# A planner that orders a decoder trunk by itself: which engines keep their order in its urgency rounds, and what it knows of PSUM

## The chip, the cores and the metric

The kernel runs on one core of one Trainium2 chip. The core has a matrix engine (TensorE, PE in the profile; its weight loads are shown apart as PEld), a vector engine (VectorE, DVE), an activation engine (ScalarE, ACT), a general engine (GpSimd, POOL) and a queue engine (SyncE, SP) that here only starts DMAs. Each has its own list of instructions and runs it in order; semaphores make one wait for another. Matmul results land in PSUM, which has eight banks of 128 partitions x 2 KB; everything else lies in SBUF. The metric is the time of one launch on the device in microseconds.

## What is computed

Two layers of a decoder trunk on a sequence of 512 with 1024 features, float32 throughout. Each layer makes one wide projection, runs three token mixers on slices of it (A: top-k sparse attention with an indexer; B: attention in a sliding window; C: stick-breaking attention), and merges them under gates:

```python
mod = c_silu @ w_ada + b_ada
shift, scale, gate = jnp.split(mod, 3, axis=-1)
u = rms_norm(x, norm_g) * (1 + scale[:, None]) + shift[:, None]
z = u @ w_in
(aq, ak, av, ag, iq, ik, iw, bq, bk, bv, bg, cq, ck, cv, cg, ma, mb, mc) = jnp.split(z, SPLIT_OFFSETS, axis=-1)
...
ya = ya.reshape(bsz, seq, A_WIDTH) * jax.nn.silu(ag)
yb = yb.reshape(bsz, seq, B_WIDTH) * jax.nn.silu(bg)
yc = yc.reshape(bsz, seq, C_WIDTH) * jax.nn.silu(cg)
merged = (jax.nn.sigmoid(ma) * (ya @ w_br_a)
          + jax.nn.sigmoid(mb) * (yb @ w_br_b)
          + jax.nn.sigmoid(mc) * (yc @ w_br_c))
return x + gate[:, None] * (merged @ w_out)
...
# stick_breaking_attention, for a block of queries:
z = jnp.einsum('bthd,bshd->bhts', qb, k).astype(jnp.float32) * (dh ** -0.5)
log_beta = jax.nn.log_sigmoid(z)
log_1m = jnp.where(strict, jax.nn.log_sigmoid(-z), 0.0)
after = lax.cumsum(log_1m, axis=3, reverse=True) - log_1m
a = jnp.where(strict, jnp.exp(log_beta + after), 0.0)
```

A final RMS norm follows the second layer.

## The kernel before

**Tiles.** Activations lie with features on partitions and the 512 tokens along the row. A float32 product is made from three matmuls in a faster format: an operand is split into a rounded part and a remainder (`uh`, `ul` for the normed input; `whi`, `wlo` for a weight chunk of 128x512; `yh`, `yl` in one tile `Y`), and high x high, low x high and high x low are summed in one PSUM bank. A weight chunk is loaded into `wstage`, rounded into `whi` (a cast, by ACT, DVE or POOL) and subtracted into `wlo` (DVE or POOL). There are three banks of the name `ps_z`, which take the projections, and five of the name `ps_s`, which take scores, transposes and mixer outputs.

**Stages of a layer.** `first_phase` projects seven column groups while `u` comes about; `v_phase` projects the values; `out_phase` multiplies by `w_out`. Between them the long middle runs several streams at once, woven by `Weave`: the three mixers in the order C, B, A, each for four pairs of heads, and beside them `prep_stream` (projections of queries, keys and gates) and `fill_stream` (merge gates and branch products), whose matmuls of 128x512 fill TensorE.

**A pair of heads in mixer C.** `stack_q` and `stack_k` take a projected bank apart into rounded halves and remainders, in pieces of 64 partitions (`Q`, `KH`, `klow`). `c_qk` makes the scores of the pair in all five `ps_s` banks; for each bank it takes the absolute value, Exp and Ln, a subtraction, a scan along the row (the order lists it as a SCALAR_TENSOR_TENSOR of 128x511, the profile as TENSOR_TENSOR_SCAN) and a last Exp, all in a tile `t`. The scan is the last reader of the bank. `softmax_tr` then transposes `t` in blocks of 128x128 on TensorE (in the profile a matmul `ps_s<-small,t`: the identity lies in `small`) into `ps_s` banks that the scans have set free, and `softmax_pv` multiplies by the values.

**What sets the order.** Nothing is emitted while this code runs: class `Recorder` records every instruction with the tiles it touches and, for many, several engines that could do it (`cast`, `both`). `price` gives a cost for each engine: `cost` is how long the engine is held, `lag` how long until the result can be used. `forward` walks through time: each engine takes the ready instruction with the lowest `prio`, `elsewhere` leaves it if another engine would end it sooner, and a tile's buffer goes to the next tile when its users are done. `latest` goes back through that plan and works out for every instruction the latest time that doesn't delay the end; that becomes its `prio` in the next round. `order` does five rounds, keeps the plan with the earliest end, and `emit` writes each engine's list in that order. All instructions are therefore emitted from line 577 (line 575 for packed pairs of matmuls), and the profile is read by tile names, not by lines.

The framework adds its own semaphore waits when the list is written, whatever the plan believed: instructions of two engines that touch one PSUM tile are kept apart by it. In `add`, the plan knows an order only between accesses that overlap and of which one writes:

```python
over = r[0] < r2[1] and r2[0] < r[1] and r[2] < r2[3] and r2[2] < r[3]
if over and j is not x and (w or w2):
    x.preds[j.i] = j
```

and `latest` hands urgency back along three kinds of link: to what an instruction needs, to the previous user of its buffer, and, for all five engines, to the instruction that stands before it in the engine's list:

```python
if x.engine in after:
    v = min(v, late[after[x.engine]] - x.hold)
```

Of the kernel before, what the change touches and what calls it, by code (L numbers as in the profile page):

```python
# [32 lines left out]
S = 512  # L33
# [214 lines left out]


class Instr:  # L250
    __slots__ = ("i", "alts", "writes", "reads", "preds", "succs", "left", "est", "tiles", "start", "end", "prio", "bound", "engine", "taken", "hold")


class Way:
# [4 lines left out]
class Recorder:  # L259
# [34 lines left out]
    def add(self, ways):  # L294
        x = Instr()
        x.i = len(self.list)
        op, args, kw = next(iter(ways.values()))
        if op == "pairs":
            named = [(("out", "in", "in")[n], v) for q in args for n, v in enumerate(q[:3])]
            opened = {id(q[0]) for q in args if q[3]}  # L300
        else:
            named = [("out" if "out" not in kw and n == 0 else n, v) for n, v in enumerate(args)] + list(kw.items())
        x.writes = [v for n, v in named if isinstance(v, View) and n in ("out", "accum_out")]
        x.reads = [v for n, v in named if isinstance(v, View) and n not in ("out", "accum_out")]
        x.preds, x.succs = {}, []
        for views, w in ((x.reads, False), (x.writes, True)):
            for v, r in [(v, r) for v in views for r in v.regions()]:
                t = v.tile
                if w and (op == "matmul" and kw["start"] or op == "pairs" and id(v) in opened):
                    r = (r[0], r[1], 0, S)  # L310
                keep = []
                for (j, r2, w2) in t.seen:
                    over = r[0] < r2[1] and r2[0] < r[1] and r[2] < r2[3] and r2[2] < r[3]
                    if over and j is not x and (w or w2):
                        x.preds[j.i] = j
                    if not (w and over and r[0] <= r2[0] and r2[1] <= r[1] and r[2] <= r2[2] and r2[3] <= r[3] and j is not x):
                        keep.append((j, r2, w2))
                t.seen = keep + [(x, r, w)]
        x.tiles = list({id(v.tile): v.tile for v in x.reads + x.writes if not v.tile.pool.fixed}.values())
        for j in x.preds.values():  # L320
            j.succs.append(x)
        x.alts = {}
        for e, (op, args, kw) in ways.items():
            x.alts[e] = self.price(x, e, op, args, kw)
        x.prio = x.i
        self.list.append(x)

    def price(self, x, engine, op, args, kw):
# [57 lines left out]
        else:  # L386
# [7 lines left out]
            else:  # L394
                c = 0.1 + 2.35e-3 * n
        y.cost, y.lag = c - self.OVERLAP[engine], c
        return y


    def forward(self):  # L400
# [1 line left out]
        dma_free, lanes = 0.0, []  # L402
        waiting = {}
        for x in self.list:
            x.left, x.est, x.bound, x.taken = len(x.preds), 0.0, len(x.tiles), False
            for t in x.tiles:
                waiting.setdefault(id(t), []).append(x)
        for c in self.classes.values():
# [5 lines left out]
        def offer(x):  # L414
            if x.left == 0 and x.bound == 0:
                for e in x.alts:
                    heapq.heappush(E[e]["pend"], (x.est, x.i))

        def give(c):
            while c.given < len(c.tiles) and c.free:  # L420
# [17 lines left out]
        while len(out) < len(self.list):  # L438
            best = None
            for name, e in E.items():  # L440
# [27 lines left out]
                        elif mine is None:  # L468
                            mine = None
                if mine is not None:  # L470
                    asked = max(free, self.list[mine[2]].est)
                    if best is None or (mine[0], asked, mine) < best[:3]:
                        best = (mine[0], asked, mine, name)
            assert best is not None, "no instruction may go"
# [23 lines left out]
            for s in x.succs:  # L498
                s.est = max(s.est, x.end + self.between(x, s))
                s.left -= 1  # L500
                offer(s)
            for t in x.tiles:
                t.users -= 1
                t.done = max(t.done, x.end + self.CROSS)
                if t.users == 0:
                    heapq.heappush(t.pool.free, (t.done, t.slot))
                    give(t.pool)
# [9 lines left out]
    def elsewhere(self, x, name, at, E):  # L517

        end = at + x.alts[name].cost
        for o, y in x.alts.items():  # L520
            if o != name:
                t = max(E[o]["free"], at, E[o]["port"] if y.port else 0.0) + y.cost
                if t < end - 1e-9:
                    return True
        return False
# [1 line left out]
    def latest(self, end, out):  # L527
# [11 lines left out]
        for x in reversed(out):  # L539
            v = late[x.i]  # L540
            took = x.end - x.start
            for s in x.succs:
                v = min(v, late[s.i] - took - self.between(x, s))
            if x.engine in after:
                v = min(v, late[after[x.engine]] - x.hold)
            for t in x.tiles:
                if id(t) in nxt:
# [57 lines left out]
def trunk(ctx, tc, xT, vecs, w_ss, w_gt, w_first, w_t, w_v, w_br, w_o, rope, consts, out):  # L605
# [268 lines left out]

    def stack_q(r, scale=None, sbuf=True):
        q = rec.tile("Q", [P, 2, S], F32R)
        for e, (a, b) in enumerate(((H0, H1), (H1, H0))):
            if scale is None:
                cast(q[a, e], r[a])
                both(q[b, e], r[a], f(q[a, e]), OP.subtract)  # L880
            else:
                cast(q[a, e], r[a], scale)
                DVE.scalar_tensor_tensor(q[b, e], r[a], scale, f(q[a, e]), op0=OP.mult, op1=OP.subtract)
        return q

# [9 lines left out]
    def stack_k(r, sbuf=True):  # L895
        kh, kl = new_kh(), klow[st["nk"] % 2]
        st["nk"] += 1
        for e, (a, b) in enumerate(((H0, H1), (H1, H0))):
            cast(kh[a, e], r[a])
            cast(kh[b, e], f(kh[a, e]))  # L900
            both(kl[a, :S], r[a], f(kh[a, e]), OP.subtract)
        cast(kl[H1, S:], f(kl[H1, :256]))
        return kh, kl

# [732 lines left out]
```

## Time and profile before

| | us |
|---|---|
| median of three runs | 1181.68 (1181.54 to 1181.86) |
| the profiled execution, launch to end | 1180.98 |
| its span, first to last instruction | 1179.1 |

| engine | busy us in the span | share | instructions |
|---|---|---|---|
| TensorE (PE) | 1166.5 | 99% | 6006 |
| VectorE (DVE) | 988.1 | 84% | 2275 |
| ScalarE (ACT) | 532.0 | 45% | 1127 |
| GpSimd (POOL) | 111.8 | 9% | 160 |

The granted TensorE clock is 0.9 of full speed or more in all 40 slices. The 16 DMA engines are 97% busy in the first 30 us and between 22% and 62% after that. The work on mixer C's pairs of heads lies at 120 to 224 us in the first layer and at 697 to 801 us in the second.

In the timeline a row has the start, the length, the engine and line, the operation, the tile written and the tiles read, the shape, and a count; in square brackets stands how long the engine was idle before it and what ended that. Matmuls overlap in the records: one of 128x512 is shown 0.39 us long, and the next starts 0.23 us after it. What TensorE really loses at a wait is therefore read from start to start, not from the idle time in brackets.

### The profile page before, as it was taken

The page shows a single profiled execution, that of the slowest core. Times are in us where ns is not written, and L with a number is a line of the kernel's source. Part 1 is how long each engine was busy: PE and PEld are TensorE (multiplying, and loading weights), DVE is VectorE, ACT ScalarE, POOL GpSimd, SP SyncE. Part 2 cuts the span into 40 slices and gives each one's busy share as a digit, 9 for nine tenths or more (in the row PEclk, how much of TensorE's full clock was granted, in tenths as well). Part 3 has the DMA queues.
Part 4 walks back from the last instruction along what each step waited for, and adds up shares of the span by engine and source line. Part 5 has one row for each costly group of instructions (what it writes and reads, how often), then busy time and mean ns, then how long its engine had stood idle before and what let it go on. Part 6 is the DMA issues. An engine that isn't in the chain of part 4 may idle for free.

```text
span 1179.1 us, 17734 instructions
## 1 busy us (share of the span) xinstructions
PE 1166.5 (99%) x6006; PEld 967.9 (82%) x6006; DVE 988.1 (84%) x2275; ACT 532.0 (45%) x1127; POOL 111.8 (9%) x160
## 2 busy tenths in 40 slices
PE   9999999999999999999999999999999999999997
PEld 8899777788878887788899987777888888877886
DVE  6977999999999887787587689999997988667765
ACT  6523667653455532632143147775443653234222
POOL 1100333310000000000000014332100000000000
PEclk9999999999999999999999999999999999999999
DMA  9644323334444454245533432333342333322343
GB/s 354 219 119 120 90 81 86 95 107 125 121 116 126 130 143 143 81 141 153 166 113 108 128 101 72 90 87 119 99 132 83 90 98 100 107 72 88 93 125 106
DMA packets 81914, 139.39 MB, mean 118 GB/s; under 512 B 10016, under 2 KB 22560, under 8 KB 81824
## 3 DMA queue, kind: packets, MB, share of 16 engines
q1 hardware_dynamic: 80672, 136.17, 39.5%
q10 hardware_dynamic: 1152, 2.10, 0.5%
q8 instruction: 47, 0.77, 0.3%
q14 instruction: 43, 0.35, 0.1%
HBM read 125.39 MB, written 4.19 MB: 110 GB/s over the span
## 4 chain that ended last, share of the span: by engine, by line
PE 81%; DVE 13%; ACT 2%; issue 2%; DMA 1%; SPq 0%; DVEq 0%; ACTq 0%
PE ps_z L577 61%; PE ps_s L577 16%; DVE t L577 5%; PE ps_s L575 4%; DVE score L577 2%; ACT t L577 1%; DVE m L577 1%; DVE wlo L577 1%; DVE Q L577 1%; DVE klow L577 1%; DMA Y<-in_w_ss 1%; DVE Y L577 0%; DVE wstage L577 0%; ACT KH L577 0%; ACT e L577 0%
## 5 line engine op out<-in xcount | busy, mean ns | idle before, releaser
L577 PE MATMUL ps_z<-uh,whi 128*128 128x512 f32 (+1 forms) x908 | 357.4, 394 | 0.0
L577 PE MATMUL ps_z<-uh,wlo 128*128 128x512 f32 (+1 forms) x908 | 353.4, 389 | 0.0
L577 PE MATMUL ps_z<-ul,whi 128*128 128x512 f32 (+1 forms) x908 | 352.5, 388 | 0.0
L577 DVE TENSOR_TENSOR wlo<-wstage,whi 128x512 fp32r<-128x512 f32 (+2 forms) x321 | 210.4, 659 | 11.0 <-ACT whi L577 2.3
L577 PEld LDWEIGHTS ps_z<-uh,whi 128*128 128x128 f32 x908 | 170.5, 188 | 35.2 <-issue 1.9
L577 PEld LDWEIGHTS ps_z<-uh,wlo 128*128 128x128 f32 x908 | 170.6, 188 | 34.6 <-issue 0.9
L577 PEld LDWEIGHTS ps_z<-ul,whi 128*128 128x128 f32 x908 | 170.7, 188 | 32.6 <-issue 0.7
L577 DVE CAST whi<-wstage 128x512 fp32r<-128x512 f32 (+2 forms) x224 | 91.3, 408 | 106.6 <-PE ps_z L577 87.5
L577 PE MATMUL ps_z<-Y,whi 128*128 128x512 f32 x384 | 119.3, 391 | 0.0
L577 ACT CAST whi<-wstage 128x512 fp32r<-128x512 f32 (+2 forms) x105 | 63.2, 602 | 109.9 <-PE ps_z L577 82.3
L577 ACT ACTIVATE e<-ps_z 128x512 f32<-128x512 f32 x68 | 40.3, 592 | 135.9 <-PE ps_z L577 135.7
L577 POOL TENSOR_TENSOR wlo<-wstage,whi 128x512 fp32r<-128x512 f32 (+2 forms) x51 | 64.8, 1271 | 382.7 <-ACT whi L577 143.8
L577 ACT ACTIVATE e<-e 128x512 f32<-128x512 f32 x96 | 59.8, 629 | 53.3 <-DVE e L577 52.8
L577 PEld LDWEIGHTS ps_z<-Y,whi 128*128 128x128 f32 x384 | 71.7, 188 | 14.7
L577 ACT ACTIVATE t<-t,nm 128x256 f32<-128x256 f32 (+3 forms) x128 | 65.1, 510 | 35.5 <-DVE nm L577 35.5
L577 PE MATMUL ps_z<-Y,wlo 128*128 128x512 f32 x192 | 74.7, 389 | 0.0
L577 ACT ACTIVATE t<-t 128x512 f32<-128x512 f32 x120 | 68.2, 625 | 13.3 <-DVE t L577 12.5
L577 PEld LDWEIGHTS ps_s<-small,t 128*128 128x128 f32 x432 | 48.8, 140 | 16.2 <-DVE t L577 5.1
L577 PE MATMUL ps_s<-small,t 128*128 128x128 f32 x432 | 58.2, 275 | 3.6 <-DVE t L577 2.5
L577 DVE MAX8 m<-score 128x8 f32<-128x256 f32 (+2 forms) x96 | 53.3, 556 | 1.1
L577 PE MATMUL ps_s<-KH,Q 128*128 128x256 f32 (+3 forms) x280 | 52.4, 309 | 0.2
L577 DVE MATCH_REPLACE8 score<-m,score 128x256 f32<-128x256 f32 (+2 forms) x96 | 52.1, 543 | 0.1
(202 smaller groups left out, 1951.5 us busy)
## 6 DMA issues: line engine op xcount, KB each, us to landing
wstage<-in_w_t SPq DMA_DIRECT2D x212, 256.0 KB, 2.7
wstage<-in_w_v SPq DMA_DIRECT2D x48, 182.0 KB, 2.4
Y<-in_w_ss SPq DMA_DIRECT2D x16, 512.0 KB, 6.2
m<-zs SPq DMA_DIRECT2D x128, 64.0 KB, 2.0
wstage<-in_w_gt SPq DMA_DIRECT2D x32, 256.0 KB, 2.6
wstage<-in_w_ss SPq DMA_DIRECT2D x32, 256.0 KB, 2.7
wstage<-in_w_o SPq DMA_DIRECT2D x32, 256.0 KB, 2.7
wstage<-in_w_first SPq DMA_DIRECT2D x16, 256.0 KB, 4.4
```

Source lines behind the costliest of these rows:

```text
L575: self.real[engine].matmul(*[real(a) for a in q[:3]], start=q[3], stop=True, skip_group_check=True)
L577: made = getattr(self.real[engine], y.op)(*[real(a) for a in y.args], **{k: real(v) for k, v in y.kw.items()})
```

## The change

Six edits, five of them in the planner:

1. `add`: two accesses to one PSUM tile, one by TensorE and one by another engine, of which one writes, are ordered even where they touch different columns (`bank and mine != ...`). Two accesses by engines other than TensorE that don't depend on each other are noted in `after` and `apart`: if they go to different engines, the later waits for the end of the earlier; on one engine they follow without a gap (`soft`).
2. `price`: an instruction of ACT or DVE on fewer than 128 partitions holds its engine for its full length and 0.02 or 0.08 us more; before, the overlap with its successor was taken off.
3. `elsewhere`: another engine's start is worked out from when the instruction is ready, not from when this engine could take it. An engine that is idle early is found more often.
4. `latest`: urgency goes back along an engine's list for TensorE and the loads (SP) only; DVE, ACT and POOL may be put in another order in the next round.
5. `latest` also goes back along the `apart` links.
6. `stack_q` and `stack_k` are recorded with all rounded halves ahead of the remainders, where the two halves of 64 partitions used to be written one after the other.

```diff
+        mine = next(iter(ways)) == "PE"
...
+                bank = t.pool.name[:3] == "ps_"
                 for (j, r2, w2) in t.seen:
                     over = r[0] < r2[1] and r2[0] < r[1] and r[2] < r2[3] and r2[2] < r[3]
-                    if over and j is not x and (w or w2):
+                    if j is not x and (w or w2) and (over or bank and mine != ("PE" in j.alts)):
                         x.preds[j.i] = j
+                    elif j is not x and bank and not mine and "PE" not in j.alts:
+                        x.after[j.i] = j
...
+            x.after.pop(j.i, None)
+        for j in x.after.values():
+            j.apart.append(x)
...
         y.cost, y.lag = c - self.OVERLAP[engine], c
+        if engine != "POOL" and o.shape[0] < P:
+            y.cost = c + (0.08 if engine == "DVE" else 0.02)
...
-            x.left, x.est, x.bound, x.taken = len(x.preds), 0.0, len(x.tiles), False
+            x.left, x.est, x.bound, x.taken = len(x.preds) + len(x.after), 0.0, len(x.tiles), False
+            x.soft = {}
...
-                    heapq.heappush(E[e]["pend"], (x.est, x.i))
+                    heapq.heappush(E[e]["pend"], (max(x.est, x.soft.get(e, 0.0)), x.i))
...
+            for s in x.apart:
+                for o in s.alts:
+                    if o != name:
+                        s.soft[o] = max(s.soft.get(o, 0.0), x.end + self.NEXT)
+                s.left -= 1
+                offer(s)
...
-                t = max(E[o]["free"], at, E[o]["port"] if y.port else 0.0) + y.cost
+                t = max(E[o]["free"], x.est, x.soft.get(o, 0.0), E[o]["port"] if y.port else 0.0) + y.cost
...
+            for s in x.apart:
+                v = min(v, late[s.i] - (x.hold if s.engine == x.engine else took + self.NEXT))
-            if x.engine in after:
+            if x.engine in after and x.engine in ("PE", "SP"):
                 v = min(v, late[after[x.engine]] - x.hold)
...
-        for e, (a, b) in enumerate(((H0, H1), (H1, H0))):
+        sides = tuple(enumerate(((H0, H1), (H1, H0))))
+        for e, (a, b) in sides:
             cast(kh[a, e], r[a])
+        for e, (a, b) in sides:
+            both(kl[a, :S], r[a], f(kh[a, e]), OP.subtract)
+        for e, (a, b) in sides:
             cast(kh[b, e], f(kh[a, e]))
-            both(kl[a, :S], r[a], f(kh[a, e]), OP.subtract)
```

Every matmul, load and vector operation of the kernel stays; their order on each engine changes, and for some the engine. TensorE's list differs in small exchanges at a few dozen places. POOL goes from 165 to 196 instructions, DVE from 2101 to 2061 and ACT from 1009 to 1018, counted in the orders. Three places are shown; the number at a row's start is its place in the engine's list, `xN` a repetition.

**TensorE in mixer C, first layer, second pair of heads**, where the transposes of `t` start between the matmuls of a projection (`ps_z`). Before:

```order
750 L577 MATMUL ps_z<-uh_607,wlo 128x512
751 L577 MATMUL ps_s<-small,t 128x128 x13
752 L577 MATMUL ps_z<-uh_206,whi 128x512
753 L577 MATMUL ps_z<-ul_221,whi 128x512
754 L577 MATMUL ps_s<-small,t 128x128 x3
755 L577 MATMUL ps_z<-uh_206,wlo 128x512
756 L577 MATMUL ps_z<-uh_268,whi 128x512
```

and now:

```order
748 L595 MATMUL ps_z<-uh_605,wlo 128x512
749 L595 MATMUL ps_s<-small,t 128x128 x11
750 L595 MATMUL ps_z<-uh_222,whi 128x512
751 L595 MATMUL ps_s<-small,t 128x128 x2
752 L595 MATMUL ps_z<-ul_232,whi 128x512
753 L595 MATMUL ps_z<-uh_222,wlo 128x512
754 L595 MATMUL ps_z<-uh_266,whi 128x512
755 L595 MATMUL ps_z<-ul_294,whi 128x512
756 L595 MATMUL ps_s<-small,t 128x128 x3
```

The group of three stood behind 13 transposes and two matmuls; it now stands behind 13 transposes and five matmuls, three later.

**VectorE in mixer C, first layer, fourth pair of heads**, from the second subtraction to the last scan (128x511). Before:

```order
279 L577 TENSOR_TENSOR m_2251<-m_2251,rt 128x512
280 L577 SCALAR_TENSOR_TENSOR t<-ps_s,t 128x511
281 L577 MEMSET t 128x1
282 L577 SCALAR_TENSOR_TENSOR t<-ps_s,t 128x512 x2
283 L577 TENSOR_TENSOR zc<-zc,m_2251 128x512
284 L577 SCALAR_TENSOR_TENSOR t<-ps_s,t 128x511
285 L577 MEMSET t 128x1
286 L577 SCALAR_TENSOR_TENSOR t<-ps_s,t 128x511
287 L577 SCALAR_TENSOR_TENSOR t<-ps_s,t 128x512 x2
288 L577 TENSOR_TENSOR KH<-zc,KH 64x512 x3
289 L577 SCALAR_TENSOR_TENSOR t<-ps_s,t 128x511
```

and now:

```order
278 L595 SCALAR_TENSOR_TENSOR t<-ps_s,t 128x512 x2
279 L595 SCALAR_TENSOR_TENSOR t<-ps_s,t 128x511 x2
280 L595 SCALAR_TENSOR_TENSOR t<-ps_s,t 128x512 x2
281 L595 SCALAR_TENSOR_TENSOR t<-ps_s,t 128x511 x2
282 L595 SCALAR_TENSOR_TENSOR t<-ps_s,t 128x512
283 L595 TENSOR_TENSOR zc<-ps_z,rt 128x512
284 L595 SCALAR_TENSOR_TENSOR t<-ps_s,t 128x511
```

The five operations on `m`, `zc` and `KH`, which belong to mixer B's keys, stood between the scans; one other stands there now, and the memsets have gone to POOL.

**VectorE in mixer C, first layer, between the projections of the first pair of heads and its first absolute value.** Before:

```order
164 L577 CAST KH<-ps_z 64x512
165 L577 CAST KH<-KH 64x512
166 L577 TENSOR_TENSOR klow_80<-ps_z,KH 64x512 x2
167 L577 MAX m_1428<-score_1256 128x8
168 L577 CAST whi<-wstage 128x512
169 L577 MATCH_REPLACE score_1256<-m_1428,score_1256 128x256
170 L577 TENSOR_TENSOR wlo<-wstage,whi 128x512
171 L577 MAX m_1457<-score_1256 128x8
172 L577 TENSOR_SCALAR mods_76<-dotg,small 128x1
173 L577 MATCH_REPLACE score_1256<-m_1457,score_1256 128x256
174 L577 MAX m_1473<-score_1256 128x8
175 L577 MATCH_REPLACE score_1256<-m_1473,score_1256 128x256
```

and now:

```order
169 L595 TENSOR_TENSOR wlo<-wstage,whi 128x512
170 L595 CAST KH<-KH 64x512
171 L595 TENSOR_TENSOR klow_80<-ps_z,KH 64x512 x2
172 L595 MAX m_1439<-score_1256 128x8
173 L595 TENSOR_TENSOR wlo<-wstage,whi 128x512
174 L595 MATCH_REPLACE score_1256<-m_1439,score_1256 128x256
175 L595 MAX m_1467<-score_1256 128x8
176 L595 MATCH_REPLACE score_1256<-m_1467,score_1256 128x256
```

One cast of `KH` out of the bank has gone to ACT. From the last score of the indexer (row 151 before, 157 now) to the first absolute value of the pair, the list has six MAX and six MATCH_REPLACE of the top-k search before, four and four now; three `whi` casts before, one now; two `wlo` before, four now.

More of the change, by code (lines that the diff above doesn't have):

```diff
@@ L250 @@
 class Instr:
-    __slots__ = ("i", "alts", "writes", "reads", "preds", "succs", "left", "est", "tiles", "start", "end", "prio", "bound", "engine", "taken", "hold")
+    __slots__ = ("i", "alts", "writes", "reads", "preds", "succs", "left", "est", "tiles", "start", "end", "prio", "bound", "engine", "taken", "hold", "after", "apart", "soft")
 class Way:
@@ L304, in add @@
         x.reads = [v for n, v in named if isinstance(v, View) and n not in ("out", "accum_out")]
-        x.preds, x.succs = {}, []
+        x.preds, x.succs, x.after, x.apart = {}, [], {}, []
+        mine = next(iter(ways)) == "PE"
         for views, w in ((x.reads, False), (x.writes, True)):
@@ L470, in forward @@
                 if mine is not None:
-                    asked = max(free, self.list[mine[2]].est)
+                    asked = max(free, self.list[mine[2]].est, self.list[mine[2]].soft.get(name, 0.0))
                     if best is None or (mine[0], asked, mine) < best[:3]:
@@ L876, in stack_q @@
         q = rec.tile("Q", [P, 2, S], F32R)
-        for e, (a, b) in enumerate(((H0, H1), (H1, H0))):
+        sides = tuple(enumerate(((H0, H1), (H1, H0))))
+        for e, (a, b) in sides:
+            cast(q[a, e], r[a], scale)
+        for e, (a, b) in sides:
             if scale is None:
-                cast(q[a, e], r[a])
                 both(q[b, e], r[a], f(q[a, e]), OP.subtract)
             else:
-                cast(q[a, e], r[a], scale)
                 DVE.scalar_tensor_tensor(q[b, e], r[a], scale, f(q[a, e]), op0=OP.mult, op1=OP.subtract)
@@ L897, in stack_k @@
         st["nk"] += 1
-        for e, (a, b) in enumerate(((H0, H1), (H1, H0))):
+        sides = tuple(enumerate(((H0, H1), (H1, H0))))
+        for e, (a, b) in sides:
             cast(kh[a, e], r[a])
+        for e, (a, b) in sides:
+            both(kl[a, :S], r[a], f(kh[a, e]), OP.subtract)
+        for e, (a, b) in sides:
             cast(kh[b, e], f(kh[a, e]))
-            both(kl[a, :S], r[a], f(kh[a, e]), OP.subtract)
         cast(kl[H1, S:], f(kl[H1, :256]))
```

## The prediction

> **What bounds the kernel now.** I read the page's busy times first, then the list of who waited for whom, then the timeline at each wait.
>
> ```profile
> PE 1166.5 (99%) x6006; PEld 967.9 (82%) x6006; DVE 988.1 (84%) x2275; ACT 532.0 (45%) x1127; POOL 111.8 (9%) x160
> PE ps_s L577 <- DVE t L577: 2.5, 7, 0.6
> PE ps_s L577 <- ACT t L577: 1.1, 2, 0.6
> PE ps_s L577 <- DVE vc L577: 0.6, 1, 0.6
> PE ps_s L577 <- ACT e L577: 0.2, 1, 0.2
> ```
>
> TensorE is busy 99% of the span, so whatever the planner does to other engines counts only where TensorE waits, at its start or behind its last matmul. The rows from the list of waits (time in total, times, longest) say where that is: nine waits for the tile `t`, which is what `softmax_tr` transposes, 3.6 us together, and one at the start. Since matmuls overlap, a wait costs more than the idle time. For five of the nine the timeline of TensorE has:
>
> ```profile
> 135.42 0.40 PE L577 MATMUL ps_z<-uh,wlo 128*128 128x512 f32 x1
> 136.46 0.41 PE L577 MATMUL ps_s<-small,t 128*128 128x128 f32 x2 [0.64 <-DVE t L577]
> 161.56 0.40 PE L577 MATMUL ps_z<-ul,whi 128*128 128x512 f32 x1
> 162.24 0.55 PE L577 MATMUL ps_s<-small,t 128*128 128x128 f32 x3 [0.29 <-DVE t L577]
> 162.54 0.48 PE L577 MATMUL ps_z<-uh,wlo 128*128 128x512 f32 x1
> 162.86 0.39 PE L577 MATMUL ps_z<-uh,whi 128*128 128x512 f32 x1
> 163.09 0.40 PE L577 MATMUL ps_z<-ul,whi 128*128 128x512 f32 x1
> 186.21 0.40 PE L577 MATMUL ps_z<-ul,whi 128*128 128x512 f32 x1
> 186.80 0.55 PE L577 MATMUL ps_s<-small,t 128*128 128x128 f32 x3 [0.19 <-DVE t L577]
> 209.11 0.27 PE L577 MATMUL ps_s<-small,t 128*128 128x128 f32 x1
> 209.93 1.10 PE L577 MATMUL ps_s<-small,t 128*128 128x128 f32 x8 [0.54 <-ACT t L577]
> 210.78 0.48 PE L577 MATMUL ps_z<-uh,whi 128*128 128x512 f32 x1
> 492.84 0.39 PE L577 MATMUL ps_z<-Y,wlo 128*128 128x512 f32 x1
> 493.47 1.33 PE L577 MATMUL ps_s<-small,t 128*128 128x128 f32 x10 [0.25 <-DVE t L577]
> 713.46 0.41 PE L577 MATMUL ps_s<-small,t 128*128 128x128 f32 x2 [0.64 <-DVE t L577]
> ```
>
> Without a wait the next start comes 0.23 us after a matmul of 128x512 (162.86 to 163.09). From 135.42 to 136.46 are 1.04 us, so 0.81 is lost; likewise 0.45 at 162.24, 0.36 at 186.80, 0.40 at 493.47. Eight transposes take from 209.93 to the next matmul at 210.78, a step of 0.11 us, so 0.71 is lost at 209.93. Each loss is the idle time and about 0.16 us of overlap; for all nine that makes 3.6 + 9 x 0.16 = **5.0 us**. The row at 713.46 shows the first of them again in the second layer, with the same idle time to the hundredth: the two layers have the same plan in this stage. Everything else on TensorE is matmuls at their pace, and the change neither removes nor adds one. So the ceiling of the gain is about 5 us, 0.4% of the span, with what the start may give on top.
>
> The stage around the first four waits, in the table by stretches (columns PE, PEld, DVE, ACT and POOL busy, clock, DMA share, GB/s), and the vector engine just ahead of it:
>
> ```profile
> 120.00:224.00 104.00, 102.34 (x554) 79.12 (x553) 102.44 (x204) 70.75 (x128) 38.93 (x56) 1.00 0.32 89
> 105.36 0.16 DVE L577 TENSOR_SCALAR iw<-ps_s 128x4 f32<-128x4 f32 x1 [0.34 <-ACT va L577]
> 105.85 0.16 DVE L577 TENSOR_SCALAR iw<-ps_s 128x4 f32<-128x4 f32 x1 [0.33 <-ACT va L577]
> 115.57 0.67 DVE L577 TENSOR_SCALAR Q<-ps_z 64x512 fp32r<-64x512 f32 x1
> 116.27 0.59 ACT L577 ACTIVATE Q<-ps_z 64x512 fp32r<-64x512 f32 x1 [0.42 <-DVE Q L577]
> 116.90 1.39 DVE L577 SCALAR_TENSOR_TENSOR Q<-ps_z,Q 64x512 fp32r<-64x512 f32 x2 [0.27 <-ACT Q L577]
> ```
>
> VectorE is as full as TensorE there, 102.4 of 104 us, so its order decides when `t` is ready. It waits for ACT where no data passes: `iw` and `va` are different columns of one bank, the two pieces of `Q` different partitions of one. The old plan took these pairs for simultaneous, so its VectorE ran late against plan. And two instructions on 64 partitions last 1.39 us, twice 0.69: the overlap that the old price takes off isn't there.
>
> **The change part by part.** The plan now counts those waits and prices (edits 1 and 2), so it places TensorE's transposes later and the scans earlier. Place by place, for the first layer:
>
> Second and third pair of heads. The group of three that waits at 162.24 moves behind three more matmuls, 3 x 0.23 = 0.69 us against a loss of 0.45. At the third pair the same group moves behind two more, 0.46 against 0.36. Gain 0.45 and 0.36, if VectorE is no later than before.
>
> First pair. TensorE's order ahead of the wait is the old one, so the gain must come from VectorE. Its durations in this stage (groups by shape, count, busy time and mean):
>
> ```profile
> L577 DVE MAX8 m<-score 128x8 f32<-128x256 f32 x14 | 5.9, 424 | 0.2
> L577 DVE MATCH_REPLACE8 score<-m,score 128x256 f32<-128x256 f32 x14 | 5.7, 410 | 0.0
> L577 DVE MATCH_VALUE_LOAD score<-m,score 128x8 f32 x22 | 1.9, 88 | 0.4
> L577 DVE CAST KH<-ps_z 64x512 fp32r<-64x512 f32 x1 | 0.7, 694 | 0.0
> L577 DVE CAST whi<-wstage 128x512 fp32r<-128x512 f32 x3 | 1.2, 411 | 0.0
> L577 DVE TENSOR_TENSOR wlo<-wstage,whi 128x512 fp32r<-128x512 f32 x8 | 5.4, 680 | 0.0
> ```
>
> Ahead of the first absolute value two MAX go (0.85), two MATCH_REPLACE with their loads (1.00), two `whi` casts (0.82), one `KH` cast (0.69), and two `wlo` come (1.36); one `whi` cast comes behind it (0.41). That is 1.6 us less in front of the scan that TensorE waits for. Of this 0.81 is needed: gain 0.81.
>
> Fourth pair. The old list has five operations of other mixers between the second subtraction and the last scan of the pair (the order above), and the timeline has their lengths:
>
> ```profile
> 202.49 0.68 DVE L577 TENSOR_TENSOR m<-m,rt 128x512 f32<-128x512 f32 x1
> 205.43 0.68 DVE L577 TENSOR_TENSOR zc<-zc,m 128x512 f32<-128x512 f32 x1
> 209.59 2.09 DVE L577 TENSOR_TENSOR KH<-zc,KH 64x512 fp32r<-64x512 f32 x3
> ```
>
> That is 0.68 + 0.68 + 2.09 = 3.45 us; one `zc` product, about 0.7, stands there now. So the last scan comes 2.7 us earlier in the list, and TensorE's transposes spread: one, then four matmuls, two, and so on, where nine stood together. Gain 0.71.
>
> The wait at 493.47 (mixer A): its transposes move behind three more matmuls, 0.69 against 0.40. In the second layer the C waits come again, 2.33, and the A wait is smaller (nine waits at 5.0 in all, less 2.33 twice and 0.40, which leaves next to nothing). Sum of the gains, if every one comes whole: 2.33 + 2.33 + 0.40 = **5.1 us**, the ceiling but for rounding.
>
> Against it stands what the new order makes late elsewhere. Two bounds from the rows: nothing, or nine new waits like the old ones, 5.0 us. A few hundred VectorE positions change, while the plan is wrong by less; I take a quarter of the old, 1.2 us, near the lower end, because the kinds of wait that surprised the old plan are the ones now counted.
>
> The start. The four warming matmuls on `vc` now stand ahead of the first sum of squares, not behind it:
>
> ```profile
> 13.54 0.67 PE L577 MATMUL ps_s<-t,nones 128*128 128x256 f32 x2 [0.62 <-DVE vc L577]
> 14.04 1.05 PE L577 MATMUL ps_s<-vc,nones 128*128 128x128 f32 x8
> 21.89 0.76 DVE L577 TENSOR_TENSOR ul<-e,uh 128x256 fp32r<-128x256 f32 x2
> 22.99 0.28 PE L577 MATMUL ps_z<-ul,whi 128*128 128x256 f32 x1
> ```
>
> That sum waits for both products `vc`, since it writes their bank; half the warming matmuls need only the first, so up to 0.45 us is won. But VectorE takes over a `wlo` of 128x384 (0.5) from POOL, and a `ul` (0.4) comes behind a long product, ahead of the `ul` at 21.89. That one was ready at 22.3 and used at 22.99: 0.7 us of slack, less the 0.45 won. Between a gain of 0.45 and a loss of 0.6 I take zero.
>
> The end. VectorE's `m` and `xm` change places with two output products, but the last chain starts at the last projection matmul, which is unmoved: nothing either way. `stack_q` and `stack_k` (edit 6) have the same instructions; their order is in the lists already counted. The loads keep their order but for a few that change places by one or two; with DMA at 0.32 in the stage they have room, at 0.97 in the first 30 us less, which is in the bounds of the start.
>
> Sum: 5.1 - 1.2 + 0 = 3.9 us less than the profiled execution's 1180.98 (span 1179.1 and 1.9 around it), 1177.1; against the median of the runs, which is 0.7 above that execution, 1181.68 - 3.9 = **1177.8 us**.
>
> **The rivals.** *The waits move on (0.24).* The plan's list scheduler never meant to wait before either, and it still did nine times. With VectorE full, earlier scans push other work back, and the lateness shows up at another transposing or at a projected bank. Half the waits or more come back: a gain of 0 to 2.3 us, about 1180.5. For it speaks 102.44 of 104; against it that top-k work has room behind mixer C, where VectorE is less full (84% over the whole span).
>
> *POOL holds VectorE up (0.12, slower).* POOL gets 31 instructions more. Its subtraction is long:
>
> ```profile
> L577 POOL TENSOR_TENSOR wlo<-wstage,whi 128x512 fp32r<-128x512 f32 x18 | 23.3, 1294 | 24.4 <-DVE KH L577 8.3 <-DVE whi L577 6.8 <-DVE wlo L577 3.3
> ```
>
> If VectorE's operations on SBUF can't run beside it, one such subtraction started just ahead of a cast or `wlo` that a scan stands behind delays the scan by up to 1.29 us. It decides once the delay exceeds the half microsecond that the transposes were moved. With one in each of the eight pairs of heads: 8 x (1.29 - 0.5) = 6.3 us of new waits, less the 3.9, +2.4: about 1184. In the trace of before POOL starts behind VectorE, as the row's releasers say, and such pairs don't overlap, which speaks for the lock but also for a plan that respects it. The Trainium skill says of this (SBUF — State Buffer, "Who interferes with whom") that the port pair is an exclusive lock and that whichever engine issues first makes the other block for the whole instruction. By that rule the sum would depend on who comes first; the trace agrees so far as POOL's idle time is ended by VectorE.
>
> *The plan guards too much.* If engines could read two halves of a bank at once, edit 1 would buy needless gaps. The row at 116.27 decides: ACT waited 0.42 us for the other 64 partitions of the bank. The Trainium skill (PSUM — Partial Sum Buffer, "PSUM bank collisions raise a hardware error") says that accesses in different quadrants of one bank may go at the same time; by it those 0.42 us would be free. Here the kernel's own semaphores make the wait, whole bank by whole bank, so the plan's rule fits the trace and the sum stands.
>
> *All comes, and the start as well (0.07):* 5.1 + 0.45, 1176.1.
>
> **How the numbers follow.** The forecast has 0.57: 1176.5 to 1179.2. A measurement of this kernel tells about 0.2% from no change, 2.4 us, so faster ends at 1179.3. The forecast and the last rival lie below it: faster 0.64; the waits moving on is within: 0.24; POOL: slower 0.12. The range of 8 in 10 goes from 1175.8, nearly the ceiling, to 1182.0, which takes in the waits moving on and leaves out POOL's case.
>
> **What would show it.** In the new list of waits the rows of TensorE for `t` should fall from 3.6 us in 9 to about 1 us in 2 or 3, with none over 0.6. In the timeline the third scan of the first pair should end a microsecond before the transposes behind it start. TensorE's busy time should fall little, since the matmuls are the same. I am wrong if the nine waits go and the time stays: then TensorE loses pace somewhere that the list of waits doesn't show, and the starts of its matmuls have to be laid side by side. I am wrong in size if more than three waits of over 0.3 us stand at new places, and wrong in sign if VectorE is idle behind POOL in the stage of mixer C.

## The result, and the profile after

| | before | after |
|---|---|---|
| median, us (6 runs each) | 1181.75 | 1174.03 |
| ratio, 95% interval | | 0.9936 (0.9923 to 0.9948) |
| the profiled execution (span), us | 1180.98 (1179.1) | 1174.64 (1172.5) |

The change makes the kernel 7.7 us faster; 3.9 us were forecast, and 1174.03 lies below the range. All runs of one kernel, here and below, lie within 2.2 us of one another, but for one of e8's five, which took 4073 us and is left out of its ratio. The page's busy times after, and the list of whom TensorE waited for (total, times, longest):

```profile
PE 1162.2 (99%) x6006; PEld 968.4 (83%) x6006; DVE 981.1 (84%) x2235; ACT 536.1 (46%) x1136; POOL 127.9 (11%) x191
PE ps_s L595 <- DMA wstage<-in_w_first: 1.4, 1, 1.4
PE ps_s L595 <- DVE epst L595: 1.0, 1, 1.0
PE ps_s L595 <- ACT e L595: 0.6, 1, 0.6
PE ps_s L595 <- DVE vc L595: 0.2, 1, 0.2
```

All nine waits for `t` are gone, and the list shows nothing in their place between start and end. TensorE's busy time fell from 1166.5 to 1162.2 us, 4.3 us, while its idle time (span less busy) fell only from 12.6 to 10.3, by 2.3. The 1.4 us row, a wait for a load at the start, is new and luck, as shown below; behind the first 20 us the idle time fell by 3.3. So over half of what went had stood in the records as busy time.

To see where, the same instruction is looked up in both timelines. First the start and the end: VectorE's first product on `Y`, which needs the first chunk of a weight load, and the last two sums on TensorE. Before, then after:

```profile
9.23 1.23 DVE L577 SCALAR_TENSOR_TENSOR Y<-Y,csr 128x1024 f32<-128x1024 f32 x1 [4.17 <-DMA Y<-in_w_ss]
1171.56 0.70 PE L577 MATMUL ps_s<-e,nones 128*128 128x256 f32 x2 [0.21 <-ACT e L577]
```

```profile
10.33 1.23 DVE L595 SCALAR_TENSOR_TENSOR Y<-Y,csr 128x1024 f32<-128x1024 f32 x1 [5.34 <-DMA Y<-in_w_ss]
1164.88 0.70 PE L595 MATMUL ps_s<-e,nones 128*128 128x256 f32 x2 [0.59 <-ACT e L595]
```

The load landed 1.1 us later in the profiled execution of the changed kernel, although the loads stand in the same order up to there in both kernels. Counted from that product to the last sums, the time went from 1162.33 to 1154.55 us, 7.78 less. This **inner time** leaves the luck of the first load out, and for the change it agrees with the medians; I use it beside them below. Now the stages between. Before (first scores ahead of mixer C, the first products with mixer B's values `vb` behind it, then the same in the second layer):

```profile
105.16 0.28 PE L577 MATMUL ps_s<-KH,Q 128*128 128x256 f32 x1
242.75 1.74 PE L575 MATMUL ps_s<-t,vb 128*64 128x256 f32 x16
682.16 0.28 PE L577 MATMUL ps_s<-KH,Q 128*128 128x256 f32 x1
819.77 1.73 PE L575 MATMUL ps_s<-t,vb 128*64 128x256 f32 x16
```

and after:

```profile
106.09 0.28 PE L595 MATMUL ps_s<-KH,Q 128*128 128x256 f32 x1
240.54 1.73 PE L593 MATMUL ps_s<-t,vb 128*64 128x256 f32 x16
678.83 0.28 PE L595 MATMUL ps_s<-KH,Q 128*128 128x256 f32 x1
813.31 1.73 PE L593 MATMUL ps_s<-t,vb 128*64 128x256 f32 x16
```

| stretch, between these rows | gain, us | of it at transposes | forecast, without the 1.2 given back |
|---|---|---|---|
| first product on `Y` to first scores | 0.17 | – | 0 |
| mixer C, first layer | 3.14 | 2.60 | 2.33 |
| rest of the first layer | 1.12 | 0.95 | 0.40 |
| mixer C, second layer | 3.13 | 2.63 | 2.33 |
| rest of the second layer | 0.22 | 0.47 | 0 |
| sum | 7.78 | 6.65 | 5.1 |

The gains are differences of the starts above (for mixer C of the first layer, from +0.93 to -2.21). The third column compares, for each of the 432 transposes, the step from the start of the matmul ahead with the median step between the same two shapes, and sums what is over by 0.025 us or more: 7.0 us at 40 starts before, 0.35 at 4 after. Ten starts lost over 0.15 us each, 5.2 together; the other thirty lost 0.025 to 0.12, 1.8 together. These thirty are in no list of waits. TensorE's timeline at one of them, before:

```profile
138.65 0.39 PE L577 MATMUL ps_z<-uh,whi 128*128 128x512 f32 x1
138.99 0.55 PE L577 MATMUL ps_s<-small,t 128*128 128x128 f32 x3
139.29 0.48 PE L577 MATMUL ps_z<-ul,whi 128*128 128x512 f32 x1
```

and the same group after:

```profile
138.11 0.39 PE L595 MATMUL ps_z<-uh,wlo 128*128 128x512 f32 x1
138.34 0.49 PE L595 MATMUL ps_s<-small,t 128*128 128x128 f32 x3
138.59 0.47 PE L595 MATMUL ps_z<-uh,whi 128*128 128x512 f32 x1
```

Before, the transposes start 0.34 us behind the matmul ahead (0.23 after) and take 0.30 (0.25 after). No bracket marks this, since the matmul ahead was still shown running. The group of all transposes, before and after (count, busy time and mean of one, idle time ahead):

```profile
L577 PE MATMUL ps_s<-small,t 128*128 128x128 f32 x432 | 58.2, 275 | 3.6 <-DVE t L577 2.5 <-ACT t L577 1.1
```

```profile
L595 PE MATMUL ps_s<-small,t 128*128 128x128 f32 x432 | 57.5, 272 | 0.0
```

The idle time shows 3.6 of the 7.0 us.

The same comparison at all other starts finds one loss that the new order has added, in mixer A of the second layer. TensorE before, then after:

```profile
1070.03 1.33 PE L577 MATMUL ps_s<-small,t 128*128 128x128 f32 x10
1071.25 0.50 PE L577 MATMUL ps_z<-uh,whi 128*128 128x512 f32 x1
```

```profile
1063.14 1.25 PE L595 MATMUL ps_s<-small,t 128*128 128x128 f32 x10
1064.54 0.50 PE L595 MATMUL ps_z<-uh,whi 128*128 128x512 f32 x1
```

Ten transposes without a wait and the step to the next matmul take 1.0 us; after, it starts 1.40 us behind the first of them, since ACT still reads the projected bank (`e<-ps_z`, 1063.91 to 1064.48). That is 0.39 us, of which 0.14 are idle time, too short for a bracket. It is the main reason why the rest of the second layer gained less than its transposes.

### The profile page after: what moved, and what is told of

Its sections match the earlier page's. It is cut to its first block, busy times and chain, and to the rows that moved or that the text cites. A ratio compares the mean times of both kernels' runs of the same rounds, so it can differ in the third digit from the quotient of the medians.

```text
span 1172.5 us, 17783 instructions
## 1 busy us (share of the span) xinstructions
PE 1162.2 (99%) x6006; PEld 968.4 (83%) x6006; DVE 981.1 (84%) x2235; ACT 536.1 (46%) x1136; POOL 127.9 (11%) x191
## 4 chain that ended last, share of the span: by engine, by line
PE 97%; issue 1%; ACT 1%; DMA 1%; DVE 1%; SPq 0%; DVEq 0%
PE ps_z L595 73%; PE ps_s L595 19%; PE ps_s L593 5%; DMA Y<-in_w_ss 1%; ACT t L595 0%; DVE Y L595 0%; DVE t L595 0%; SPq L595 0%; ACT e L595 0%; ACT ps_s L595 0%; ACT whi L595 0%; DVE wlo L595 0%; DVE xm L595 0%; DVE vc L595 0%; DVEq L1653 0%
## 5 line engine op out<-in xcount | busy, mean ns | idle before, releaser
L595 DVE TENSOR_TENSOR wlo<-wstage,whi 128x512 fp32r<-128x512 f32 (+2 forms) x331 | 218.4, 661 | 12.0 <-ACT whi L595 1.9
L595 DVE CAST whi<-wstage 128x512 fp32r<-128x512 f32 (+2 forms) x231 | 94.6, 410 | 114.0 <-PE ps_z L595 95.9
L595 ACT CAST whi<-wstage 128x512 fp32r<-128x512 f32 (+2 forms) x112 | 67.7, 604 | 132.8 <-PE ps_z L595 106.9
L595 POOL TENSOR_TENSOR wlo<-wstage,whi 128x512 fp32r<-128x512 f32 (+2 forms) x41 | 52.2, 1273 | 143.8 <-DVE whi L595 60.2
```

The costliest lines, as they stand in the source:

```text
L595: made = getattr(self.real[engine], y.op)(*[real(a) for a in y.args], **{k: real(v) for k, v in y.kw.items()})
```

## The experiments

Twelve kernels ran, each beside runs of the kernel before on the same chip. "Inner" is the time from the first product on `Y` to the last sums in the one profile of each, against 1162.33 before. It lies within 0.7 us of the medians but for e4, e6 and e10, where the two differ by 0.9 to 1.3.

| kernel | median (us against before) | ratio, 95% interval | inner against before |
|---|---|---|---|
| the change | -7.7 | 0.9936 (0.9923 to 0.9948) | -7.8 |
| e1 edit 4 alone | -0.7 | 0.9992 (0.9983 to 1.0001) | -1.0 |
| e2 all but edit 4 | -4.4 | 0.9962 (0.9950 to 0.9975) | -4.4 |
| e3 before, TensorE's list new | +5.2 | 1.0044 (1.0031 to 1.0056) | +5.1 |
| e4 changed, TensorE's list old | +4.8 | 1.0039 (1.0025 to 1.0053) | +3.5 |
| e5 all but edits 1 and 5 | -4.9 | 0.9960 (0.9948 to 0.9972) | -4.6 |
| e6 all but edit 2 | -5.3 | 0.9959 (0.9947 to 0.9972) | -4.3 |
| e7 all but edit 6 | -8.5 | 0.9930 (0.9917 to 0.9944) | -7.8 |
| e8 all but edit 3 | -8.0 | 0.9931 (0.9918 to 0.9945) | -7.7 |
| e9 edits 1, 2, 4, 5 | -7.6 | 0.9936 (0.9924 to 0.9949) | -7.7 |
| e10 changed, VectorE's list kept in `latest` | -4.7 | 0.9962 (0.9949 to 0.9974) | -3.7 |
| e11 changed, ACT's list kept in `latest` | -8.2 | 0.9933 (0.9919 to 0.9947) | -7.7 |
| e12 all but the `elif` of edit 1, and 5 | -6.1 | 0.9951 (0.9939 to 0.9964) | -6.3 |

My theory at first was that of the prediction: TensorE waited because the plan did not know the pairs on one bank and the 64-row prices (edits 1 and 2). The rival: the freed urgency (edit 4) is the gain.

**e1: edit 4 alone**, against the kernel before.

```diff
-            if x.engine in after:
+            if x.engine in after and x.engine in ("PE", "SP"):
```

> The kernel before with edit 4 alone: urgency goes back along the lists of TensorE and the loads only; banks and 64-row prices as the old plan knows them. Knowledge theory (TensorE waited because the plan did not know the pairs on one bank and the 64-row prices): the plan still believes the scans come earlier than they do, so most of the nine waits for t stay, more than 2.5 of 3.6 us in the list of waits, and the time is within 1.5 us of before. Urgency theory (the old order of VectorE was frozen by handing urgency back along its own list, and freeing it is the gain): the waits for t fall under 1 us and the time is 5 to 8 us below before. If each brings a part, 2 to 5 us below.

TensorE's waits in it:

```profile
PE ps_s L589 <- DVE t L589: 1.6, 6, 0.3
PE ps_s L589 <- DVE zc L589: 1.6, 2, 0.8
PE ps_s L589 <- ACT t L589: 0.6, 1, 0.6
```

Waits for `t` fall from 3.6 to 2.2 us, where the first theory expected more than 2.5 to stay and the rival less than 1, and two for `zc` come, 1.6 us. A plan that is free to reorder but works with wrong prices trades one wait for another. A gain can't be told from none (the interval includes 1). The rival falls as the whole cause.

**e2: all but edit 4.**

```diff
-            if x.engine in after and x.engine in ("PE", "SP"):
+            if x.engine in after:
```

> The changed kernel with edit 4 undone: the plan knows banks and 64-row prices, urgency goes back along all five lists as before. Knowledge theory: the waits for t stay away and the time is within 1.5 us of the changed kernel, 6 to 8 us below before. Urgency theory: the plan sees the lateness but can't reorder VectorE against its last round; waits for t of 2.5 us and more, and a time within 2 us of before. If each brings a part, 2 to 5 us below before.

Mixer C has no wait left. All that stands between start and end is in mixer A, at three places (timeline):

```profile
490.53 1.33 PE L595 MATMUL ps_s<-small,t 128*128 128x128 f32 x10 [0.28 <-DVE t L595]
492.96 0.50 PE L595 MATMUL ps_z<-uh,whi 128*128 128x512 f32 x1 [1.10 <-ACT e L595]
1067.43 1.39 PE L595 MATMUL ps_s<-small,t 128*128 128x128 f32 x10 [0.97 <-ACT t L595]
```

These are 0.44, 1.34 and 1.13 us from start to start, 2.9 of the 3.3 us by which its inner time is over that of the change. Knowledge alone brings over half, and gives back at a new place what it can't order there. Both theories were half right: each brings a part.

**e3 and e4: TensorE's list exchanged.** Is the gain TensorE's, whose transposes stand later, or VectorE's, whose scans stand earlier? e3 is the kernel before with TensorE's list rearranged into the order of the planner's edits, the other lists word for word as before; e4 the changed kernel with TensorE's list in the old planner's order. Read from the traces, e3's list is not that of the change (210 of 6006 places differ, all but two of them in mixer C's stages) but that of e7 and e9 below, two versions without edit 6 that are as fast as the change; e4's differs in 150 places from that of before.

```diff
+MOVED = {25: [60, 61, 63, 64, 73], 79: [184, 151, 152, 154, 155, 157, 158, 160, 161, 163, 164, 166, 167, 169, 170], ...
...
+        for n, ids in MOVED.items():
+            assert sorted(lists["PE"][n:n + len(ids)]) == sorted(ids)
+            lists["PE"][n:n + len(ids)] = ids
```

> The kernel before with TensorE's list alone in the order of the changed planner (57 small exchanges); VectorE, ACT, POOL and the loads stand as before. Theory that TensorE's own order is enough (transposes two or three matmuls later): gain at the second and third pairs and at mixer A, 2 x (0.45 + 0.36) + 0.40, about 2 us, the first pair's 0.8 stays. Theory that VectorE's order is what counts: the scans end when they did, the waits move from one transposing to another, and the time is within 1 us of before or above it.

> The changed kernel with TensorE's list alone in the old planner's order (51 small exchanges back); the other engines stand as changed. Theory that VectorE's order is what counts: most of the gain stays, 5 us or more below before, with waits for t under 1.5 us. Theory that TensorE's own order is what counts: waits for t of 2 us or more, and less than half of the gain, under 4 us below before.

Both are some 5 us slower than before, which neither theory had forecast for e4; for e3 the second had only "or above it". In e3 TensorE's new list asks for what the old lists of the other engines deliver late:

```profile
139.17 0.55 PE L623 MATMUL ps_s<-small,t 128*128 128x128 f32 x3 [0.40 <-ACT t L623]
210.44 1.20 PE L623 MATMUL ps_s<-small,t 128*128 128x128 f32 x9 [1.21 <-ACT t L623]
```

In e4 the old list has the scores of the second pair two projection matmuls earlier; they need a bank that VectorE's `e` reads last, and VectorE now has `e` later:

```profile
149.34 0.47 PE L641 MATMUL ps_s<-KH,Q 128*128 128x256 f32 x2 [2.40 <-DVE e L641]
```

It comes again in the second layer. Part of e4's time is the clock's. Its trace has the granted clock at half for 3.4 us behind the first of these waits (columns: PE, PEld, DVE, ACT and POOL busy, clock, DMA share, GB/s):

```profile
151.30:154.70 3.40, 3.40 (x10) 2.66 (x9) 2.14 (x5) 3.12 (x7) 0.00 (x0) 0.50 0.21 66
```

Matmuls of 128x512 start 0.43 us apart there in place of 0.23, which costs about 1.7 us of the profiled run. All five runs of e4 have a mean granted clock of 0.995 to 0.997, those of before 0.998 or 0.999. Even without the 1.7 us the inner time is 1.8 over that of before.

The same list of TensorE is 5 us slower than before beside the old lists (e3) and 8 us faster beside new ones (e7, e9). So the gain does not lie in TensorE's list alone, and by e4 not in the other lists alone, but in that they fit each other.

**e5 and e6: which knowledge.** e5 takes the banks out (edits 1 and 5; the loop of edit 5 is not shown), e6 the price (edit 2).

```diff
-                    if j is not x and (w or w2) and (over or bank and mine != ("PE" in j.alts)):
+                    if j is not x and (w or w2) and over:
...
-                    elif j is not x and bank and not mine and "PE" not in j.alts:
-                        x.after[j.i] = j
```

```diff
-        if engine != "POOL" and o.shape[0] < P:
-            y.cost = c + (0.08 if engine == "DVE" else 0.02)
```

> The changed kernel without the knowledge of shared banks (edits 1 and 5 undone); the 64-row price, the freed urgency and edits 3 and 6 stay. If bank knowledge is what ends the waits of mixer C: waits for t of 1.5 us and more come back as in the kernel with edit 4 alone, and the time is within 3 us of before. If the 64-row price is enough: waits for t under 0.7 us, time 6 to 8 us below before. If each brings a part: 3 to 6 below.

> The changed kernel without the 64-row price (edit 2 undone); all else stays. If bank knowledge is enough: time within 1 us of the changed kernel, 6.5 to 8 us below before, waits for t under 0.7 us. If the price is what counts: waits for t of 1.5 us and more, time within 3 us of before. If each brings a part: 3 to 6 below.

Each brings a part, and of different waits. Without banks there is hardly a wait in mixer C, but there are others where TensorE meets VectorE on a bank (e5; the one for `zc` is there in both layers):

```profile
58.60 0.57 PE L591 MATMUL ps_s<-whi,uh 128*128 128x364 f32 x2 [0.30 <-DVE zc L591]
331.16 1.16 PE L591 MATMUL ps_s<-KH,Q 128*128 128x256 f32 x8 [0.41 <-DVE mx L591]
```

Without the price the first pair's wait is back, 0.69 from start to start in each layer where it was 0.81, and the scores of the second pair wait 0.83 (e6):

```profile
136.25 0.41 PE L593 MATMUL ps_s<-small,t 128*128 128x128 f32 x2 [0.52 <-DVE t L593]
148.22 0.51 PE L593 MATMUL ps_s<-KH,Q 128*128 128x256 f32 x2 [0.58 <-DVE e L593]
```

**e7, e8 and e9: edits 3 and 6.** e7 has `stack_q` and `stack_k` as before, e8 `elsewhere`, e9 both.

```diff
-                t = max(E[o]["free"], x.est, x.soft.get(o, 0.0), E[o]["port"] if y.port else 0.0) + y.cost
+                t = max(E[o]["free"], at, E[o]["port"] if y.port else 0.0) + y.cost
```

> The changed kernel with stack_q and stack_k recorded in the old way (edit 6 undone). If the gain is the plan's, which orders these pieces by itself from the banks it knows: within 1 us of the changed kernel, 7 to 8 us below before. If writing all halves out of the bank first shortens VectorE's path to the scans: waits for t come back at the pairs of mixer C, and 1 to 4 us of the gain go.

> The changed kernel with the old start time of another engine in elsewhere (edit 3 undone). TensorE's list is the same row by row; about 285 places of VectorE's differ, and POOL does five operations more. If TensorE's list and the waits of mixer C carry the gain: within 0.7 us of the changed kernel. If finding an idle engine more often is a part of it: new waits for t or e, and 1 us or more of the gain goes.

> The kernel before with edits 1, 2, 4 and 5 only: banks, price and freed urgency, without elsewhere and the stack order. If these three carry all of it: 7.5 to 8.7 us below before, as the kernel without the stack order was, and no wait for t in the list. If edit 3 and edit 6 help each other: less than 7 us below.

The inner times of all three are within 0.1 us of the change's, though their lists differ from its: e7 and e9 in 208 places of TensorE's, e8 in VectorE's alone. Edits 3 and 6 bring nothing that can be seen; the medians of e7 and e8 are lower only by as much as the start varies (the last section).

**e10 and e11: whose freed list.** Edit 4 freed DVE, ACT and POOL. The waits of e2 ended mostly with ACT.

```diff
-            if x.engine in after and x.engine in ("PE", "SP"):
+            if x.engine in after and x.engine in ("PE", "SP", "DVE"):
```

> The changed kernel, but urgency also goes back along VectorE's list (edit 4 undone for VectorE alone). With all five lists kept, the waits of mixer A stood (2.9 us at three places) and 3.3 us of the gain were missing. If VectorE's frozen order is the cause: waits of 2 us or more in mixer A, time 3 to 5 us below before. If it is ACT's: no such waits, 7 us or more below before.

> The changed kernel, but urgency also goes back along ACT's list (edit 4 undone for ACT alone). The waits of mixer A ended with ACT (a reciprocal's exponent e, a tile t): if ACT's frozen order is the cause, 2 us or more of waits in mixer A, time 3 to 5 us below before. If it is VectorE's: no such waits, 7 us or more below before.

It is VectorE's: keeping it costs 4.1 us of inner time, or 3.1 by the medians, keeping ACT's nothing. All of the 4.1 lies in mixer A of the first layer: 1.50 and 0.89 from start to start ahead of the matmuls at 490.67 and 492.62, and the rest again the clock, at half for 3.4 us behind these waits:

```profile
492.50:495.90 3.40, 3.28 (x11) 2.79 (x12) 1.35 (x4) 1.61 (x4) 0.00 (x0) 0.50 0.00 0
```

The timelines show why an ACT that is named last is not the cause. In e10, ACT and VectorE ahead of the transposes at 490.67, from VectorE's first maximum on:

```profile
482.22 0.69 DVE L595 CUSTOM_DVE_ANT_0 t<-ps_s,score 128x512 f32<-128x512 f32 x1 [0.23 <-PE ps_s L593]
486.91 0.28 DVE L595 TENSOR_SCALAR nm<-mx 128x4 f32<-128x4 f32 x2
487.11 0.72 ACT L595 ACTIVATE t<-t,nm 128x512 f32<-128x512 f32 x1 [9.14 <-DVE nm L595]
490.67 1.31 PE L595 MATMUL ps_s<-small,t 128*128 128x128 f32 x10 [1.34 <-ACT t L595]
```

In the change, VectorE from the same first maximum on:

```profile
483.17 0.69 DVE L595 CUSTOM_DVE_ANT_0 t<-ps_s,score 128x512 f32<-128x512 f32 x1 [0.16 <-PE ps_s L593]
485.44 0.16 DVE L595 TENSOR_SCALAR nm<-mx 128x4 f32<-128x4 f32 x1
487.54 0.17 DVE L595 TENSOR_SCALAR nm<-mx 128x4 f32<-128x4 f32 x1
```

A pair of heads has two softmaxes; each needs the maxima of four blocks (`mx`) before the negative maximum `nm`, and ACT's exponents wait for `nm`. With VectorE's order handed back from round to round, the maxima of both heads stay mixed (two of 128x512, two of 128x384, and so on), and both `nm` come 4.7 us behind the first maximum; ACT waited for them. Freed, VectorE takes the four maxima of one head first and then one of the other's, and the first `nm` comes 2.3 us behind the first maximum.

**e12: which half of the bank knowledge.** The loop of edit 5 goes as well.

```diff
-                    elif j is not x and bank and not mine and "PE" not in j.alts:
-                        x.after[j.i] = j
```

> The changed kernel without the second half of the bank knowledge: pairs of engines other than TensorE on one bank are not noted (the elif of edit 1, and edit 5, undone); TensorE against the others stays known, whole bank by whole bank. With both halves gone 2.8 us of the gain were missing, in waits for mx and zc. If those pairs (iw and va, the halves of Q) are the half that counts: 1.5 us or more missing, 4.5 to 6 us below before. If TensorE's side counts: within 1 us of the changed kernel.

1.4 us of inner time go with it, against 3.2 for both halves (e5): this half is worth somewhat under half. That the other is worth the rest is argued; it was not taken out alone. The waits for `zc` come back here, and two starts of scores behind ACT's `e` that lose 0.25 us each, as before the change; those for `mx` don't.

## Why the prediction was wrong in size

**The ceiling** was the step that failed. The prediction put the loss at the list's nine waits, 3.6 us and 0.16 for the overlap of each, "5.0 us", and took everything else on TensorE for matmuls at their pace. The nine were measured rightly: 0.81, 0.45, 0.36, 0.71 and 0.40 in the first layer and 5.1 in all, and they all went. But 1.9 us more were lost at 31 other transposes, in pieces under 0.2 us, which the overlap hides from the list, and 1.6 of them went. Two starts of scores behind ACT's `e`, hidden in the same way, went as well; the first of them before:

```profile
107.74 0.40 PE L577 MATMUL ps_z<-ul,whi 128*128 128x512 f32 x1
108.21 0.45 PE L577 MATMUL ps_s<-KH,Q 128*128 128x384 f32 x1
```

That is a step of 0.47 us in place of 0.23, in each layer. Together 5.1 + 1.6 + 0.5 = 7.2, and with the new loss of 0.4 at 1064.54, 6.8. Of the other 1.0 of 7.8, 0.17 came at the start; the rest lies in still smaller differences and is not put down to single instructions. With it falls the sentence that TensorE's busy time would fall little: it fell by 4.3 us.

**What the new order makes late elsewhere** was taken as 1.2 us; 0.4 was found, and no new wait for `t` stands in the list. The size had a basis, since with edits 1 and 5, edit 2 or edit 4 left out 3.2 to 3.4 us come back (e5, e6, e2), partly at new places: `zc` and `mx`, the scores behind `e`, mixer A. Only with all of these edits does the list show none. A ceiling 3.1 too low and new losses put 0.8 too high are the 3.9 us by which the forecast fell short.

**The reasons** held in part. The prediction gave the gain to edits 1 and 2. They do clear mixer C (e2), but 3.3 us hang on edit 4, on VectorE's list, at mixer A; there the prediction named only TensorE's move, 0.69 against 0.40. With the old lists of the other engines TensorE's new order costs 5 us (e3). At the second pair the move was enough even there (the group of three, still later in that list, starts without a wait, and 0.09 is lost ahead of it), but at mixer A the same ten transposes lost 0.40 at their start and 0.30 within. So the reason held at one place and failed at the other, and the clause "if VectorE is no later than before" belonged to the whole list.

**First pair**: 1.6 us less ahead of the first absolute value. VectorE's timeline, before and after:

```profile
127.95 0.69 DVE L577 TENSOR_SCALAR t<-ps_s 128x512 uint32<-128x512 uint32 x1
```

```profile
127.01 1.89 DVE L595 TENSOR_SCALAR t<-ps_s 128x512 uint32<-128x512 uint32 x3
134.66 2.32 DVE L595 TENSOR_TENSOR_SCAN t<-ps_s,t 128x511 f32<-128x511 f32 x2
136.19 0.38 PE L595 MATMUL ps_s<-small,t 128*128 128x128 f32 x2
```

It comes 0.94 us earlier although the stage began 0.93 later (106.09 against 105.16): 1.9, near the 1.6. The third scan, the first of the two at 134.66, ends about 135.9, 0.3 us ahead of the transposes at 136.19, not the whole microsecond that I had asked for.

**The start** was taken as zero. By the first projection matmul, 17.77 before and 18.50 after, the new warming order had won 0.37 us of the 0.45 thought possible (8.54 and 8.17 us behind the first product on `Y`); 0.17 are left at the first scores. **The end** is as forecast: the last two sums wait 0.59 us for ACT's `e` in place of 0.21, but the sums ahead of them no longer lose 0.28.

**The rivals.** POOL did not hold VectorE up: among VectorE's waits at 105 to 245 us none names POOL, though POOL's busy time went from 111.8 to 127.9 us. That list alone would not tell, since VectorE behind POOL shows as a longer instruction and not as idle time. There is one such in the change, far from the scans (VectorE, then POOL):

```profile
991.75 1.15 DVE L595 TENSOR_TENSOR wlo<-wstage,whi 128x512 fp32r<-128x512 f32 x1
991.06 1.29 POOL L595 TENSOR_TENSOR klow<-zc,KH 64x512 fp32r<-64x512 f32 x1 [16.49 <-DVE KH L595]
```

This `wlo` takes 1.15 us where the mean of its kind is 0.69. Between 105 and 245 us one VectorE instruction is longer than its kind by more than 0.1, by 0.16 at 229.41. So the mechanism of this rival exists, and the plan kept it away from the scans. It is the lock of which the Trainium skill speaks (SBUF — State Buffer, "Who interferes with whom"): there, too, the engine that issues second is the one that blocks. "The waits move on" describes the reduced kernels e1, e2 and e10, not the change. Whole-bank waits between engines, which the plan's rule assumes, are borne out: without that rule 3.2 us go (e5).

## What to carry to other kernels

A busy engine's list of waits counts only what sticks out behind its overlapping records; lay starts side by side, against the median step of the same shapes, before calling a sum of waits a ceiling. In a planner that iterates, right prices and the freedom to act on them are worth more together (7.7 us here) than one after the other (4.4 and 0.7): with the freedom alone waits move, with the prices alone some waits are only moved to where the order is frozen. The engine that a wait names last (ACT) may be innocent; follow its own idle time one step further back before changing its order.

## What was not expected of the hardware

The first weight load landed at different times though the first 13 rows of SP's list are the same in all fourteen kernels and the load is the fourth of them: VectorE's first product on it starts between 8.55 us (e11, below) and 10.33 us (the change) in the fourteen profiles, and the whole kernel moves with it. Five versions whose inner times agree within 0.1 us (the change, e7, e8, e9, e11) have medians from 1173.0 to 1174.0.

```profile
8.55 1.22 DVE L595 SCALAR_TENSOR_TENSOR Y<-Y,csr 128x1024 f32<-128x1024 f32 x1 [3.57 <-DMA Y<-in_w_ss]
```

Why the load is late at times was not tried. The profile of before, at 9.23, was on the early side, so the two profiled executions alone (6.3 us apart) would have understated the change.

The granted clock falls to half for 3.4 us in the middle of two of the fourteen profiles, shortly behind TensorE's idle 2.40 us (e4) and 1.34 and 0.65 us (e10). The waits of before, at most 0.64 us, and those of e3, at most 1.21, had no such effect, and in e4 the second wait of 2.40 us had none. A wait can therefore cost more than its own length; what sets it off was not tried.
